# The weights of the first w1 chunk behind w2, placed 32 bytes nearer to x modulo 256

## The chip, the cores and the metric

The kernel runs on one core of a Trainium2 chip. Its time is the device time of one execution in microseconds (us); the runs shown are compared by their median. The engines of a core work side by side: TensorE (PE; its loading of weights is shown apart, as PEld), VectorE (DVE), ScalarE (ACT), GpSimd (POOL) and SyncE (SP), which issues the transfers.

## What is computed

Two transformer layers over 256 tokens of width 2048 in float32. The first layer's mixer is stick-breaking attention, the second's a sparse attention in three branches; behind each mixer stands the same kind of MLP with a hidden width of 8192. The MLPs are what this change touches:

```python
def sqrelu_mlp(h, w1, w2):
    return jnp.square(jax.nn.relu(h @ w1)) @ w2
...
h = h + sqrelu_mlp(rms_norm(h, mlp_norm_g[layer]), mlp_w1[layer], mlp_w2[layer])
```

## The kernel before

**Products in three parts.** Float32 products are made from parts. Each operand is split into a rounded part `hi` and the rest `lo`, and a product is the sum of three: hi by hi, lo of the activations by hi of the weights, and hi of the activations by lo of the weights. `split` (line 129 on) makes the parts of a chunk of weights: a chunk is 128 x 1024 elements (512 KB), ScalarE copies it into `hi` (line 133), VectorE subtracts (line 135). Activations of the running layer stand in `xs`, with the parts `xhi` and `xlo` side by side; the MLP's hidden values stand in `yhi` and `ylo`.

**Two forms of a chunk.** `chunk_T` (matmul at line 185) loads the weights' parts into TensorE and streams x beside them, 256 columns at a time: 16 matmuls with hi, then 8 with lo. `chunk_N` (line 155) does it the other way round: activations are loaded, and the weights' parts are streamed, 512 columns at a time, 12 matmuls a chunk. `chunk_S` (line 246) is a variant of the second with 256 columns that forms sums of blocks first (one level of Strassen's scheme), 21 matmuls a chunk. In all forms TensorE loads the stationary operand of the next matmul while the moving operand of the running one streams.

**Place modulo 256.** A buffer of parts has `KC * NB + PAD` = 1024 + 64 elements in each partition, 4352 bytes, that is 17 x 256, and a row of `xs` has 2048 bytes. So all buffers of a kind have one place modulo 256 bytes, whichever buffer and whichever column block it is. In the memory map of the compiled program x, yhi, ylo and the starts of the buffers for hi and lo all lie at 128 modulo 256. The offset given to `split` moves the parts inside their buffers: `NEAR` (0 elements, for chunk_N) leaves them at 128, at x's own place; `FAR` (16 elements, 64 bytes, for chunk_T) puts them at 192; `SUM` (48 elements, for chunk_S) at 64.

**Order of the MLP.** `mlp` goes through four groups `fg` of 2048 hidden values. `group1` computes h times w1 for the group: four blocks `fb` of 512 hidden values, each with eight chunks in the form chunk_T, so 192 matmuls of 256 columns a block and 768 a group. `group2` adds the group's part of the product with w2: 24 chunks in the form chunk_N and 8 in the form chunk_S between them. Group 0's w1 stands behind the mixer's output projection, and transposes for the next activations run between its chunks (lines 303 and 352). Groups 1 to 3 stand directly behind the w2 products of the group before. This is done twice, once in each layer, so there are six turns from w2 to w1.

**What sets the order.** Each engine goes through its instructions in the order of the program; buffers come free in turn (five for raw weights, four each for hi and lo). Transfers of weights are issued on SP's queue in the order of the chunks.

Of the kernel before, what the change touches and what calls it, by code (L numbers as in the profile page):

```python
# [18 lines left out]
D = 2048  # L19
KD = D // P  # L20
NB = 512
# [4 lines left out]
KC = 2  # L26
# [13 lines left out]
def hybrid_kernel(  # L40
# [62 lines left out]
    def spawn(gen, rate, wait=0.0, first=False):  # L103
        beside.insert(0 if first else len(beside), [gen, rate, -wait])

    def pump():
        if beside:
            b = beside[0]
            b[2] += b[1] / KC
            while b[2] >= 1:  # L110
                b[2] -= 1
                y = next(b[0], b)
                if y is b:
                    beside.remove(b)
                if y:
                    break
# [6 lines left out]

    PAD = 64
    NEAR, FAR, SUM = 0, 16, 48

    def split(raw, o=(NEAR, NEAR)):
        n = KC * NB  # L130
        view = lambda t, a: t[:, a:a + n].rearrange("p (k n) -> p k n", k=raw.shape[1])
        hi = view(whi.tile([P, n + PAD], F32R, tag="hi", name="hi"), o[0])
        nc.scalar.activation(hi, raw, AF.Copy)  # L133
        lo = view(wlo.tile([P, n + PAD], F32R, tag="lo", name="lo"), o[1])
        nc.vector.tensor_tensor(lo, raw, hi.bitcast(F32), op=OP.subtract)  # L135
# [9 lines left out]
    def load_split(*where, o=(NEAR, NEAR)):  # L145
        return split(load(*where), o)

    def bank(pool, tag):
        return pool.tile([P, NB], F32, tag=tag, name=tag)
# [27 lines left out]
    def chunk_T(ps, src, k0, n0, first, last, nk=KC, o=None):  # L177

        nm = KC * NB // P // nk
        hi, lo = src if isinstance(src, tuple) else load_split(src, k0, nk, n0, nm * P, o=o or (FAR, FAR))  # L180
        tiles = [(kk, m) for kk in range(nk) for m in range(nm)]

        def mm(w, x, kk, m, s, e):
            o = ps[m // 2][:, (m % 2) * T:(m % 2 + 1) * T]
            nc.tensor.matmul(o, w[:, kk, m * P:(m + 1) * P], x[:, k0 + kk, :], start=s, stop=e, skip_group_check=True)  # L185

        for kk, m in tiles:
            mm(hi, xhi, kk, m, first and kk == 0 and m % 2 == 0, False)
            mm(hi, xlo, kk, m, False, False)
        pump()  # L190
        for kk, m in tiles:
            mm(lo, xhi, kk, m, False, last and kk == nk - 1)
        pump()

    def proj_T(ps, src, n0, nk=KC, o=None):
        for k0 in range(0, KD, nk):
            chunk_T(ps, src, k0, n0, k0 == 0, k0 + nk == KD, nk, o)

    def proj_Th(src, n0):

# [10 lines left out]
    def chunk_S(ps, src, k0, n0, first, last, ahi, alo, shi, slo, koff=0):  # L211
# [9 lines left out]
        hi, lo = [  # L221
            wsum.tile([P, 3 * W + PAD], F32R, tag=n, name=n, bufs=1)[:, SUM:SUM + 3 * W] for n in ("shi", "slo")
        ]
# [62 lines left out]
    def split_evac(hi, lo, src, scale=None):  # L286

        if scale is None:
            nc.scalar.activation(hi, src, AF.Copy)  # L289
            nc.vector.tensor_tensor(lo, src, hi.bitcast(F32), op=OP.subtract)  # L290
        else:
            nc.scalar.activation(hi, src, AF.Copy, scale=scale)
            nc.vector.scalar_tensor_tensor(
                lo, src, scale, hi.bitcast(F32), op0=OP.mult, op1=OP.subtract
            )
# [44 lines left out]
    def make_rstd(layer):  # L340
        s = small.tile([P, NT], F32, tag="ms", name="ms")
        nc.vector.tensor_reduce(s, ssq_t[layer], axis=AX.X, op=OP.add)
        nc.vector.tensor_scalar(s, s, 1.0 / D, EPS, op0=OP.mult, op1=OP.add)
        r = small.tile([P, NT], F32, tag="rstd", name="rstd")
        nc.gpsimd.tensor_tensor(r, s, neghalf[:, :NT], op=OP.pow)
        return r

    def bcast_rows(rstd):

        ps = bank(att, "att")  # L350
        for t in range(NT):
            nc.tensor.transpose(ps[:, t * P:(t + 1) * P], rstd[:, t:t + 1].to_broadcast([P, P]), ident)
        return ps
# [36 lines left out]
    def mlp(l, layer, junk, done, last=None):  # L390
        w1, w2 = mlp_w1[l], mlp_w2[l]
        ss = junk.tile([P, 2, KD // 2, 4, P], F32R, name="ss", bufs=1)
        row = junk.tile([P, T], F32, name="row", bufs=1)

        def rows():
            yield
            pb = bcast_rows(make_rstd(layer))
            nc.scalar.activation(row, pb[:, :T], AF.Copy)

        def group1(fg, pools):  # L400

            for fb in range(D // NB):
                ps = [bank(*pools[fb % 2]) for _ in range(NB // P // 2)]
                proj_T(ps, w1, fg * D + fb * NB)
                k, n = fb * (NB // P), NB // P
                a = junk.tile([P, n, T], F32, tag="pre", name="pre", bufs=1)
                for j in range(0, n, 2):
                    nc.vector.scalar_tensor_tensor(
                        a[:, j:j + 2, :], ps[j // 2].rearrange("p (m t) -> p m t", m=2), 0.0,
                        row.unsqueeze(1).to_broadcast([P, 2, T]), op0=OP.max, op1=OP.mult,  # L410
                    )
                s = junk.tile([P, n, T], F32, tag="sq", name="sq", bufs=1)
                nc.scalar.activation(s, a, AF.Square)
                nc.scalar.activation(yhi[:, k:k + n, :], s, AF.Copy)
                nc.vector.tensor_tensor(ylo[:, k:k + n, :], s, yhi[:, k:k + n, :].bitcast(F32), op=OP.subtract)

                sv = s.rearrange("p (j kk) t -> p j kk t", kk=2)
                a1, a2 = [[sv[:, :, kk, t * P:(t + 1) * P] for kk in (1, 0)] for t in range(NT)]
                q = junk.tile([P, 2, 4, P], F32, tag="sums", name="sums", bufs=1)
                nc.vector.scalar_tensor_tensor(q[:, :, 0, :], a2[0], -1.0, a2[1], op0=OP.mult, op1=OP.subtract)  # L420
                nc.vector.tensor_tensor(q[:, :, 2, :], a1[0], a2[0], op=OP.subtract)
                nc.vector.tensor_tensor(q[:, :, 1, :], a2[1], q[:, :, 2, :], op=OP.subtract)
                nc.vector.tensor_tensor(q[:, :, 3, :], a1[1], q[:, :, 1, :], op=OP.subtract)
                split_evac(ss[:, 0, k // 2:k // 2 + 2], ss[:, 1, k // 2:k // 2 + 2], q)

        def group2(fg, plain, strassen, end):

            NK = KD // KC
            order, si = [], 0
            for i in range(3 * NK):  # L430
                order.append(((0, 1, 3)[i // NK], i % NK))
                if si < NK and i >= (3 + 1.75 * si if end else 4 + 2.25 * si):
                    order.append((2, si))
                    si += 1
            for nb, i in order:
                k0 = fg * KD + i * KC
                args = (w2, k0, nb * NB, i == 0, i == NK - 1, yhi, ylo)
                if nb == 2:
                    if i == 0:
                        bs, s = banks_S(*strassen)  # L440
                    chunk_S(s, *args, ss[:, 0], ss[:, 1], koff=fg * KD)
                    if i == NK - 1:
                        add_S(nb, bs, s, junk)
                        if end:
                            for n in range(3):
                                done(n, strassen)
                    continue
                if i == 0:
                    ps = [bank(*plain) for _ in range(NT)]
                out = last is not None and end and nb == 3  # L450
                chunk_N(ps, w2, k0, nb * NB, i == 0, i == NK - (2 if out else 1), yhi, ylo, koff=fg * KD,
                        by_token=out and i == NK - 1)
                if i == NK - 1:
                    if out:
                        add_out(nb, ps, last)
                        return
                    add_h(nb, ps)
                    if end and nb == 3:
                        done(nb, plain)

        spawn(rows(), 1)
        A, B = (acc, "acc"), (att, "att")
        for fg in range(DFF // D):
            end = fg == DFF // D - 1
            group1(fg, ((A, B), (B, A))[fg % 2])
            group2(fg, *((A, B), (B, A))[fg % 2], end)
# [211 lines left out]
    with tc.tile_pool(name="nsa", bufs=2) as ap, ExitStack() as last:  # L678
# [255 lines left out]
        for i in range(2):  # L934
            cT = cp.tile([P, G, T], F32, tag="cT", name="cT", bufs=1)
            for b in range(2):
                ps = proj_Th(w_in, C0 + i * NB + b * T)
# [61 lines left out]
        for g in range(G):  # L999
            ps = [bank(acc, "acc") for _ in range(NT)]  # L1000
# [16 lines left out]
            ps = proj_N(w_in, g * NB)  # L1017
# [46 lines left out]
```

## Time and profile before

| | |
|---|---|
| median of three runs | 2195.87 us (2195.24 to 2197.57) |
| profiled execution | 2196.84 us, span 2195.1 us |
| mean granted clock of TensorE | 0.999 of full speed |
| TensorE busy | 2186.2 us in 14482 matmuls |
| VectorE, ScalarE busy | 1484.1 us, 1164.7 us |
| read from HBM | 401.83 MB |

The span goes from the first to the last instruction; the profiled execution's own time is 1.74 us longer. Times in the rows below are counted from the span's start. A matmul is shown with its whole duration, from issue to the landing of its result, and the next begins long before it ends; how fast a run of matmuls goes is read from the distance between their starts.

### The profile page before, as it was taken

To read this page: it belongs to the slowest core of one execution; us is meant where nothing else is said; L and a number is where in the kernel's file an instruction comes from. 1 tells how busy PE (TensorE), PEld (TensorE's weight loads), DVE (VectorE), ACT (ScalarE), POOL (GpSimd) and SP (SyncE) were. 2 spreads that over 40 slices of the span, in tenths; PEclk is the share of its full clock that TensorE was granted. 3 is DMA by queue.
4 is the path that set the end of the run, shared out by engine and by line. 5 is a ranking of instruction groups with operands and counts; after the bars stand their busy time and mean duration, and the time that the engine had idled before them with its cause. 6 is when DMAs were issued, how large, how long until landed. Compare 5 with 4: busy or idle time off the path is not lost.

```text
span 2195.1 us, 36040 instructions
## 1 busy us (share of the span) xinstructions
PE 2186.2 (100%) x14482; PEld 1997.6 (91%) x14482; DVE 1484.1 (68%) x1968; ACT 1164.7 (53%) x1537; POOL 42.5 (2%) x75
## 2 busy tenths in 40 slices
PE   9999999999999999999999999999999999999999
PEld 9999988998998998899898888889989989989998
DVE  4655556677667667767777877755776676677676
ACT  5555565455445454445546666655544454554453
POOL 0000000000000000000000011000000000000000
PEclk9999999999999999999999999999999999999999
DMA  6655555665665765665667554456657656656654
GB/s 222 204 180 172 156 182 176 186 197 186 200 190 175 215 187 178 215 185 184 203 182 222 163 144 139 139 164 186 190 189 206 182 192 202 191 183 205 189 186 160
DMA packets 260784, 406.28 MB, mean 185 GB/s; under 512 B 13188, under 2 KB 91912, under 8 KB 260616
## 3 DMA queue, kind: packets, MB, share of 16 engines
q1 hardware_dynamic: 259800, 403.52, 60.0%
q8 instruction: 113, 1.85, 0.3%
q10 hardware_dynamic: 816, 0.46, 0.1%
q14 instruction: 55, 0.45, 0.1%
HBM read 401.83 MB, written 2.10 MB: 184 GB/s over the span
## 4 chain that ended last, share of the span: by engine, by line
PE 99%; DVE 0%; POOL 0%; ACT 0%; issue 0%; DVEq 0%; ACTq 0%; POOLq 0%
PE acc L155 31%; PE acc L185 26%; PE att L185 16%; PE att L155 13%; PE acc L246 4%; PE att L246 4%; PE att L896 1%; PE att L303 1%; PE att L888 0%; PE att L889 0%; PE att L890 0%; PE att L583 0%; PE att L631 0%; PE att L842 0%; PE att L844 0%; PE att L843 0%
## 5 line engine op out<-in xcount | busy, mean ns | idle before, releaser
L133 ACT ACTIVATE hi<-raw 128x1024 fp32r<-128x1024 f32 x687 | 726.5, 1059 | 740.3 <-PE acc L155 227.1
L135 DVE TENSOR_TENSOR lo<-raw,hi 128x1024 fp32r<-128x1024 f32 x687 | 836.0, 1221 | 395.6 <-ACT hi L133 374.7
L185 PE MATMUL acc<-xs,hi 128*128 128x256 f32 x3312 | 420.4, 280 | 1.9 <-ACT hi L133 1.9
L185 PEld LDWEIGHTS acc<-xs,hi 128*128 128x128 f32 x3312 | 400.1, 189 | 2.7 <-ACT hi L133 2.1
L185 PE MATMUL att<-xs,hi 128*128 128x256 f32 x2048 | 259.8, 280 | 0.0
L155 PE MATMUL acc<-hi,yhi 128*128 128x512 f32 x640 | 250.7, 392 | 0.0
L155 PE MATMUL acc<-hi,ylo 128*128 128x512 f32 x640 | 249.3, 390 | 0.0
L185 PEld LDWEIGHTS att<-xs,hi 128*128 128x128 f32 x2048 | 248.3, 189 | 0.3
L185 PE MATMUL acc<-xs,lo 128*128 128x256 f32 x1656 | 226.5, 279 | 0.0
L185 PEld LDWEIGHTS acc<-xs,lo 128*128 128x128 f32 x1656 | 207.4, 189 | 0.0
L155 PE MATMUL acc<-hi,xs 128*128 128x512 f32 x704 | 177.2, 392 | 0.0
L155 PE MATMUL acc<-lo,yhi 128*128 128x512 f32 x640 | 172.4, 390 | 0.0
L155 PEld LDWEIGHTS acc<-hi,xs 128*128 128x128 f32 x704 | 130.3, 188 | 26.6
L155 PE MATMUL att<-hi,yhi 128*128 128x512 f32 x380 | 148.2, 390 | 0.0
L155 PE MATMUL att<-hi,ylo 128*128 128x512 f32 x380 | 147.9, 389 | 0.0
L155 PEld LDWEIGHTS acc<-lo,yhi 128*128 128x128 f32 x640 | 119.5, 188 | 24.9 <-issue 0.4
L155 PEld LDWEIGHTS acc<-hi,ylo 128*128 128x128 f32 x640 | 120.2, 188 | 23.3 <-DVE ylo L290 0.2
L155 PEld LDWEIGHTS acc<-hi,yhi 128*128 128x128 f32 x640 | 120.2, 188 | 23.3 <-ACT yhi L289 0.2
L185 PE MATMUL att<-xs,lo 128*128 128x256 f32 x1024 | 140.4, 280 | 0.0
L185 PEld LDWEIGHTS att<-xs,lo 128*128 128x128 f32 x1024 | 128.7, 189 | 0.0
L220 DVE TENSOR_TENSOR ts<-raw 128x512 f32<-128x512 f32 x64 | 44.3, 692 | 115.6 <-DMA raw<-in_mlp_w_dram 115.5
L133 ACT ACTIVATE hi<-ts 128x1024 fp32r<-128x1024 f32 x64 | 67.8, 1059 | 87.8 <-DVE ts L226 41.8
(290 smaller groups left out, 2501.3 us busy)
## 6 DMA issues: line engine op xcount, KB each, us to landing
raw<-in_mlp_w_dram SPq DMA_DIRECT2D x512, 512.0 KB, 3.9
raw<-in_sb_w_qkv_dram SPq DMA_DIRECT2D x95, 512.0 KB, 3.8
raw<-in_nsa_w_in_dram SPq DMA_DIRECT2D x50, 512.0 KB, 3.8
raw<-in_sb_w_out_dram SPq DMA_DIRECT2D x32, 512.0 KB, 3.9
raw<-in_nsa_w_in_dram SPq DMA_DIRECT2D x64, 256.0 KB, 3.4
raw<-in_nsa_w_out_dram SPq DMA_DIRECT2D x32, 512.0 KB, 3.7
w1t<-in_nsa_cmp_w_dram SPq DMA_DIRECT2D x8, 512.0 KB, 4.9
h<-in_x_dram SPq DMA_DIRECT2D x8, 256.0 KB, 4.1
```

What stands on the lines that cost most here:

```text
L133: nc.scalar.activation(hi, raw, AF.Copy)
L135: nc.vector.tensor_tensor(lo, raw, hi.bitcast(F32), op=OP.subtract)
L155: mm = lambda a, b, k, t, s, e: nc.tensor.matmul(ps[t], a[:, k, t * P:(t + 1) * P], b, start=s, stop=e)
L185: nc.tensor.matmul(o, w[:, kk, m * P:(m + 1) * P], x[:, k0 + kk, :], start=s, stop=e, skip_group_check=True)
L220: nc.vector.tensor_tensor(ts[:, :2, :], flat[:, W:3 * W].rearrange("p (a n) -> p a n", a=2), b12, op=OP.subtract)
L246: nc.tensor.matmul(ps[i], a, w, start=s, stop=e, skip_group_check=True)
L303: nc.tensor.transpose(ps[:, j * T + t * P:j * T + (t + 1) * P], h[:, t, (kp + j) * P:(kp + j + 1) * P], ident)
L896: nc.tensor.transpose(ptp[:w, j * P:(j + 1) * P], src(j), ident)
```

## The change

`proj_T` can now give its first chunk another offset, `TURN`: 8 elements, 32 bytes, in place of 64. `group1` asks for it in block 0 of groups 1 to 3. So in six chunks of the whole kernel (three in each layer), hi and lo begin at 160 modulo 256 in place of 192, with x at 128. The chunks behind it, and all others, keep their offsets. No instruction is added or left out.

```diff
-    NEAR, FAR, SUM = 0, 16, 48
+    NEAR, FAR, TURN, SUM = 0, 16, 8, 48
...
-    def proj_T(ps, src, n0, nk=KC, o=None):
+    def proj_T(ps, src, n0, nk=KC, turn=False):
         for k0 in range(0, KD, nk):
-            chunk_T(ps, src, k0, n0, k0 == 0, k0 + nk == KD, nk, o)
+            o = TURN if turn and k0 == 0 else FAR
+            chunk_T(ps, src, k0, n0, k0 == 0, k0 + nk == KD, nk, (o, o))
...
                 ps = [bank(*pools[fb % 2]) for _ in range(NB // P // 2)]
-                proj_T(ps, w1, fg * D + fb * NB)
+                proj_T(ps, w1, fg * D + fb * NB, turn=fg > 0 and fb == 0)
```

## Rows read from the trace of the kernel before

**Rows 1.** The page, part 1: busy time, share of span, number of instructions.
```profile
PE 2186.2 (100%) x14482; PEld 1997.6 (91%) x14482; DVE 1484.1 (68%) x1968; ACT 1164.7 (53%) x1537; POOL 42.5 (2%) x75
```

**Rows 2.** Table of waits, TensorE: who was waited for, total, times, longest.
```profile
PE acc L185 <- ACT hi L133: 1.9, 1, 1.9
PE att L489 <- POOL ident masks.py:199: 1.6, 1, 1.6
PE att L761 <- DVE hs L757: 0.9, 1, 0.9
PE att L796 <- DVE kc L792: 0.5, 1, 0.5
PE acc L508 <- ACT hi L501: 0.2, 1, 0.2
```

**Rows 3.** Chain that ended last, by time: start, duration, what, number of matmuls.
```profile
421.39 21.76 PE att L185 x192
...
571.76 22.61 PE att L185 x192
...
2083.42 22.61 PE acc L185 x192
```

**Rows 4.** Windows of w1 stages, line 185: length, busy (number), granted clock, DMA.
```profile
412.96:486.51 73.55, 73.55 (x649) 73.51 (x648) 1.00 0.66 193
571.60:662.05 90.45, 90.45 (x768) 90.41 (x767) 1.00 0.65 190
...
1505.68:1579.23 73.55, 73.55 (x649) 73.52 (x648) 1.00 0.65 194
...
2015.42:2105.87 90.45, 90.45 (x768) 90.41 (x767) 1.00 0.65 189
```

**Rows 5.** Timeline at the first turn: start, duration, engine, line, count.
```profile
570.69 1.07 PE L155 MATMUL acc<-lo,yhi 128*128 128x512 f32 x4
...
571.60 2.05 PE L185 MATMUL att<-xs,hi 128*128 128x256 f32 x16
573.48 1.11 PE L185 MATMUL att<-xs,lo 128*128 128x256 f32 x8
```

**Rows 6.** Timeline of TensorE in the first w1 stage.
```profile
400.92 2.05 PE L185 MATMUL acc<-xs,hi 128*128 128x256 f32 x16
402.80 1.11 PE L185 MATMUL acc<-xs,lo 128*128 128x256 f32 x8
...
406.93 0.60 PE L303 MATMUL att<-ident,h 128*128 128x128 f32 x4
...
410.10 1.98 PE L185 MATMUL acc<-xs,hi 128*128 128x256 f32 x16
411.92 1.07 PE L185 MATMUL acc<-xs,lo 128*128 128x256 f32 x8
```

**Rows 7.** Timeline of TensorE at the end of the kernel, line 163.
```profile
2190.08 0.40 PE L163 MATMUL att<-lo,yhi 128*128 128x256 f32 x2
2190.32 0.40 PE L163 MATMUL att<-hi,yhi 128*128 128x256 f32 x2
2190.56 0.40 PE L163 MATMUL att<-hi,ylo 128*128 128x256 f32 x2
```

**Rows 8.** The page, part 5: splitting a chunk; busy, mean ns, idle before.
```profile
L133 ACT ACTIVATE hi<-raw 128x1024 fp32r<-128x1024 f32 x687 | 726.5, 1059 | 740.3 <-PE acc L155 227.1
L135 DVE TENSOR_TENSOR lo<-raw,hi 128x1024 fp32r<-128x1024 f32 x687 | 836.0, 1221 | 395.6 <-ACT hi L133 374.7
```

**Rows 9.** Window of the first w1 stage, all engines: PE, PEld, DVE, ACT, POOL.
```profile
412.96:486.51 73.55, 73.55 (x652) 73.55 (x649) 48.58 (x54) 38.32 (x39) 0.00 (x0) 1.00 0.66 193
```

**Rows 10.** Window of 32 matmuls of compress, line 750.
```profile
1199.17:1202.95 3.78, 3.78 (x32) 3.73 (x31) 1.00 0.66 164
```

**Rows 11.** Timeline of TensorE, a projection of the first layer behind chunk_N.
```profile
153.74 1.07 PE L155 MATMUL acc<-lo,xs 128*128 128x512 f32 x4
154.64 2.05 PE L185 MATMUL acc<-xs,hi 128*128 128x256 f32 x16
156.53 1.11 PE L185 MATMUL acc<-xs,lo 128*128 128x256 f32 x8
```

**Rows 12.** Timeline of TensorE behind the products with tri and ones.
```profile
103.05 0.28 PE L618 MATMUL att<-sh,tri 128*128 128x256 f32 x1
103.16 0.28 PE L619 MATMUL att<-sl,tri 128*128 128x256 f32 x1
103.28 1.98 PE L185 MATMUL acc<-xs,hi 128*128 128x256 f32 x16
105.09 1.07 PE L185 MATMUL acc<-xs,lo 128*128 128x256 f32 x8
106.00 1.18 PE L185 MATMUL acc<-xs,hi 128*128 128x256 f32 x9
```

**Rows 13.** Timeline of TensorE behind the products with the values.
```profile
114.48 1.19 PE L185 MATMUL acc<-xs,lo 128*128 128x256 f32 x8
115.51 2.05 PE L185 MATMUL acc<-xs,hi 128*128 128x256 f32 x16
117.39 1.11 PE L185 MATMUL acc<-xs,lo 128*128 128x256 f32 x8
```

**Rows 14.** Timeline of TensorE, first products of w2 behind two w1 stages.
```profile
486.51 0.40 PE L155 MATMUL acc<-hi,yhi 128*128 128x512 f32 x1
...
487.89 0.39 PE L155 MATMUL acc<-hi,yhi 128*128 128x512 f32 x1
...
662.05 0.40 PE L155 MATMUL att<-hi,yhi 128*128 128x512 f32 x1
...
663.44 0.39 PE L155 MATMUL att<-hi,yhi 128*128 128x512 f32 x1
```

## The prediction

> **What bounds the kernel now.** I read the page's busy times first: TensorE is busy for 2186.2 of 2195.1 us [rows 1]. The table of waits then says whether that is real. All that TensorE's matmuls waited for another engine is 1.9, 1.6, 0.9, 0.5 and 0.2 us, 5.1 us together [rows 2]. So nothing that feeds TensorE can give more than those 5 us, and the kernel's time is the number of matmuls times the distance between the starts of two of them. I call that distance the pace. It has to be read from starts, not from the duration of one matmul, because matmuls overlap.
>
> The third view is the chain that ended last, in order of time [rows 3]. One block of w1 is always 192 matmuls of 256 columns at line 185. The reader is to compare equal work: blocks of the first w1 stage take 21.76 us (113.3 ns a matmul), blocks of a later stage 22.61 us (117.8 ns). [...]
>
> The fourth view is the timeline where a pace begins. At the turn from w2 to w1 the first 16 matmuls behind the last product of w2 take 573.48 - 571.60 = 1.88 us, 117.5 ns each [rows 5]: the slow pace is there from the first chunk, and by [rows 4] it stays for all 32 chunks. In the first stage the same line starts slow as well (400.92 to 402.80, 16 in 1.88 us), but transposes stand between its chunks; after them it is fast, 16 in 1.82 us (410.10 to 411.92) [rows 6], and it stays fast to the end of that stage. The pace is thus a rhythm that the stage inherits: it survives as long as identical chunks follow each other, and a disturbance can change it.
>
> **The change part by part.** No instruction is added, removed or moved: the same 24 matmuls, one Copy on ScalarE and one subtraction on VectorE for each chunk. What changes is the start of hi and lo in six chunks (three turns in each of two layers): 160 modulo 256 in place of 192, with x at 128. The distance between the weights that are loaded and the x that streams beside them goes from 64 to 32 bytes; the other 31 chunks of each stage keep 64.
>
> *Does the distance matter at all?* The rows say yes. At the very end of the kernel matmuls of the same shape run with a distance of 0 (line 163, weights and moving data both at 128). Their pairs start at 2190.08, 2190.32 and 2190.56 [rows 7]: 120 ns each, constant, at the same clock. At a distance of 64 the steady paces are 113.3 and 117.8. [...]
>
> [...]
>
> *Work on ScalarE and VectorE.* A chunk's Copy is 1059 ns and its subtraction 1221 ns [rows 8] for the same 1024 elements at either place. I cost the move at nothing. The cover: in a fast stage a chunk lasts 24 x 113.3 = 2.72 us, and ScalarE is busy 38.32 and VectorE 48.58 of 73.55 us [rows 9]. Were the cover gone, only what exceeds 2.72 us would show; that is over a microsecond away. Transfers: a faster stage asks for its 512 KB every 2.72 us in place of 2.83. The first stages do exactly that, at 193 GB/s against 190, without TensorE idling [rows 4, 9].
>
> *The chunk with the new distance.* The trace has no long run at a distance of 32. The nearest are the matmuls of compress (line 750), whose weights step through eight distances, 32 among them: 32 of them in a row take 3.78 us, 118.1 ns on the mean [rows 10]. So I bound the six chunks by 113.3 and 120 ns and take 117.8, what they have now: 0 us, between -6 x 24 x 4.45 ns = -0.6 us and 6 x 24 x 2.2 ns = +0.3 us.
>
> *The 31 chunks behind it.* This is the only term of size. If the return from 32 to 64 leaves the stage at the fast pace, a stage saves 31 x 24 x 4.45 ns = 3.31 us, and six save 19.9 us; take some 0.1 us off for matmuls in which the new pace settles (after transposes it takes two or three). That is 19.8 us. From below it is 0, if the 117.8 ns come back.
>
> Which end is nearer? Entries into line 185 in the trace: straight from a long run of 512-column products the pace is slow each time (571.60 [rows 5], 154.64 [rows 11], and all six turns by [rows 4]). But entered without a pause from a few 256-column matmuls at a distance of 0, it is fast: 16 in 1.81 us (103.28 to 105.09), then the 8 of lo in 0.91 [rows 12]. After a pause it is mostly fast [rows 6], sometimes slow: behind the value products 16 take 1.88 us (115.51 to 117.39) [rows 13]. So the long 512-column run is the one entry that never gives 113.3 ns, and what the change does is to put 24 matmuls of 256 columns with another distance between that run and the stage. That is nearer to [rows 12] than to [rows 5], and I take the fast end, without being sure of it: a disturbance re-rolls the rhythm, and [rows 13] shows that it can fall on 117.8.
>
> *Behind the stage.* The first six products of w2 take 487.89 - 486.51 = 1.38 us behind a fast stage and 663.44 - 662.05 = 1.39 us behind a slow one [rows 14]. So the gain isn't given back there, and w2's own pace does not depend on it.
>
> **Sum.** 2196.84 us for the profiled execution, less 19.8, is 2177.0. The median of the runs shown is 2195.87, 0.97 lower, so I forecast 2195.87 - 19.8 = 2176.1 us.
>
> **The rivals.**
> *The 117.8 ns come back.* [...] For it: six of six turns, and the entry behind a pause in [rows 13]. Against it: [rows 12]. Price: the bounds of the six chunks alone, -0.6 to +0.3 us: 2195.9 us. Chance 0.25.
>
> *The change doesn't do what it says*: the place has no effect on pace and the two paces come from something else, such as the phase of two clocks. Then even the six chunks keep 117.8: 2195.9 us. [...] Against it stands the 120 ns at distance 0 [rows 7]. Chance 0.05.
>
> *Some turns flip, others not.* Each is worth 3.3 us; three of six give 2195.9 - 9.9 = 2186.0. For it: pauses of the same kind in [rows 6] and [rows 13] end differently. Against it: all six turns behave alike in [rows 4]. Chance 0.07.
>
> *Slower:* the chunk at 32 leaves a third rhythm, as slow as line 163's 120 ns, and the stage inherits it. Price: 6 x 31 x 24 x 2.2 ns = 9.8 us, 2205.7 us; it decides from a pace of 118.8 on, where 4464 matmuls lose 4.4 us. For it: 120 ns holds steadily at the end of the kernel [rows 7]. Against it: at a distance of 64 the long stages show two paces only, and these 31 chunks have a distance of 64. Chance 0.04.
>
> **How the numbers follow.** My forecast has 0.59: 2174.6 to 2178.5 by its own bounds (all of the first chunk's gain on the best run, against some late settling and the spread of runs). The partial case adds 0.07 and reaches to 2190. To leave out no more than 2 in 10 the range has to take in the return of the 117.8 ns, 2195.9 with the spread of the runs: 2174.6 to 2197.4. 0.2% is 4.4 us, about what a measurement of this kernel can tell from no change. Faster: 0.59 + 0.07 = 0.66. Same: 0.25 + 0.05 = 0.30. Slower: 0.04.
>
> **What would show it.** In the chain of the changed kernel the later w1 blocks of 192 should take 21.76 us, and their windows about 87.1 us in place of 90.45. The timeline at a turn should show 16 matmuls in about 1.81 us from the second or third chunk on. Blocks of 22.61 us mean that the first rival holds; a first chunk at an unchanged 117.8 ns would speak for the second; 23 us and more for the last. The w2 stages and the first w1 stage must be unchanged; if their lengths move, my account of what the change touches is wrong. The prediction fails if the rhythm behind the chunk is set by something that 24 matmuls at another distance don't alter.

## The result, and the profile after

The changed kernel takes 2177.06 us (median of four runs, 2175.53 to 2177.46), the kernel before, run beside it, 2196.72 us (2195.24 to 2199.73): a ratio of 0.9907, 95% interval 0.989 to 0.9925, so 0.9% faster. The forecast was 2176.1 us. The profiled execution has a span of 2175.3 us against 2195.1, 19.8 us less.

The page's busy times, part 1, of the changed kernel: the numbers of instructions are the same, and TensorE is busy for 20.8 us less [rows 1].

```profile
PE 2165.4 (100%) x14482; PEld 1976.4 (91%) x14482; DVE 1482.8 (68%) x1968; ACT 1163.2 (53%) x1537; POOL 42.6 (2%) x75
```

The chain that ended last, in order of time, at the first and the last turn. All lines are one higher than before: line 186 is the former 185.

```profile
570.38 21.88 PE att L186 x192
592.26 21.76 PE acc L186 x192
614.02 21.76 PE att L186 x192
635.78 21.76 PE acc L186 x192
...
1998.71 21.88 PE att L186 x192
...
2064.11 21.76 PE acc L186 x192
```

Every block that took 22.61 us [rows 3] now takes 21.76 us, but for the first of each stage, which holds the chunk at 32 bytes. The windows of the w1 stages, line 186 alone:

```profile
411.46:485.01 73.55, 73.55 (x649) 73.51 (x648) 1.00 0.66 193
570.22:657.38 87.16, 87.16 (x768) 87.12 (x767) 1.00 0.67 199
742.48:829.64 87.16, 87.16 (x768) 87.12 (x767) 1.00 0.67 197
...
1998.55:2085.71 87.16, 87.16 (x768) 87.12 (x767) 1.00 0.65 193
```

All six stages are 87.16 us long. Two of the six windows of before stand in [rows 4]; these are the other four:

```profile
747.15:837.60 90.45, 90.45 (x768) 90.41 (x767) 1.00 0.65 190
922.69:1013.15 90.46, 90.46 (x768) 90.41 (x767) 1.00 0.64 187
...
1664.33:1754.78 90.45, 90.45 (x768) 90.41 (x767) 1.00 0.66 190
1839.87:1930.33 90.46, 90.46 (x768) 90.41 (x767) 1.00 0.65 190
```

So each stage is 3.29 or 3.30 us shorter than before, 19.76 us together. The first w1 stage, which the change does not touch, is 73.55 us as before; the granted clock is 1.00 in all these windows, before and after. That accounts for the 19.8 us of the span. (Outside the stages this execution was 1.4 us ahead at the first turn and lost 1.3 us again later: 0.9 us in the w2 products behind the second layer's first w1 stage, most of the rest behind the last stage.)

The timeline of TensorE at the first turn, to be held against [rows 5]:

```profile
569.31 1.08 PE L156 MATMUL acc<-lo,yhi 128*128 128x512 f32 x4
570.22 2.06 PE L186 MATMUL att<-xs,hi 128*128 128x256 f32 x16
572.12 1.11 PE L186 MATMUL att<-xs,lo 128*128 128x256 f32 x8
573.06 1.98 PE L186 MATMUL att<-xs,hi 128*128 128x256 f32 x16
574.88 1.07 PE L186 MATMUL att<-xs,lo 128*128 128x256 f32 x8
```

The chunk at 32 bytes takes 573.06 - 570.22 = 2.84 us for its 24 matmuls, 118.3 ns each: a little more than the 117.8 ns that it had. The chunk behind it goes at the short pace at once, 16 in 574.88 - 573.06 = 1.82 us. So nothing is gained where the place was changed; all is gained in the 31 chunks behind it, whose place was not changed.

### The profile page after: what moved, and what is told of

Same layout as the page of the kernel before. It is cut to its first block, busy times and chain, and to the rows that moved or that the text cites. A ratio compares the mean times of both kernels' runs of the same rounds, so it can differ in the third digit from the quotient of the medians.

```text
span 2175.3 us, 36040 instructions
## 1 busy us (share of the span) xinstructions
PE 2165.4 (100%) x14482; PEld 1976.4 (91%) x14482; DVE 1482.8 (68%) x1968; ACT 1163.2 (53%) x1537; POOL 42.6 (2%) x75
## 4 chain that ended last, share of the span: by engine, by line
PE 97%; DMA 1%; DVE 1%; issue 0%; POOL 0%; ACT 0%; DVEq 0%; ACTq 0%; POOLq 0%
PE acc L156 29%; PE acc L186 26%; PE att L186 16%; PE att L156 13%; PE acc L248 4%; PE att L248 3%; DMA raw<-in_mlp_w_dram 1%; PE att L898 1%; DVE lo L136 1%; PE att L305 1%; PE att L890 0%; PE att L891 0%; PE att L892 0%; PE att L585 0%; PE att L633 0%; PE att L844 0%
## 5 line engine op out<-in xcount | busy, mean ns | idle before, releaser
L186 PE MATMUL acc<-xs,hi 128*128 128x256 f32 x3312 | 413.5, 277 | 1.9 <-ACT hi L134 1.9
L186 PEld LDWEIGHTS acc<-xs,hi 128*128 128x128 f32 x3312 | 393.5, 188 | 2.8 <-ACT hi L134 2.1
L186 PE MATMUL att<-xs,hi 128*128 128x256 f32 x2048 | 253.3, 276 | 0.0
L186 PEld LDWEIGHTS att<-xs,hi 128*128 128x128 f32 x2048 | 242.2, 188 | 0.3
```

## The experiments

Three theories stood at first. A "break" is here a short stretch of matmuls that differ from those around them. A (rhythm): 113.3 and 117.8 ns are two rhythms of the same matmuls, and any break can move the stage from one to the other. B (place): 32 bytes is the better distance in itself. C (seam): what counts is how the first weights are loaded beside the last product of w2. Each run was made once, beside the kernel before on the same chip, whose time is given in brackets; the verdicts rest on the length of the six stages in the trace, which agree within 0.02 us in all runs but one.

**All chunks at 32 bytes.**

```diff
-            o = TURN if turn and k0 == 0 else FAR
+            o = TURN if turn else FAR
...
-                proj_T(ps, w1, fg * D + fb * NB, turn=fg > 0 and fb == 0)
+                proj_T(ps, w1, fg * D + fb * NB, turn=fg > 0)
```

> All 32 chunks of the six w1 stages behind w2 have the 32 byte distance, not the first alone. Theory A (rhythm): the two paces at a distance of 64 are two rhythms of one thing, 32 is no better distance in itself and only breaks the rhythm. Then the whole stage keeps the pace that the first chunk of the changed kernel has, 2.84 us for 24 matmuls (118.2 ns): 90.8 us a stage, about 2199 us in all. Theory B (place): 32 is the better place. Then the stage is at 113.3 ns or less, 87.0 us a stage, 2176.5 us or less.

2198.34 us (2193.31). The window of the first stage behind a turn, line 186, and the chain of this kernel, second and third block of that stage:

```profile
570.23:661.11 90.88, 90.88 (x768) 90.83 (x767) 1.00 0.64 189
...
593.11 22.72 PE acc L186 x192
615.83 22.72 PE att L186 x192
```

118.3 ns from the first matmul of a stage to the last, more than before the change. B is refuted: 32 bytes is no better distance, it only leads to something better at 64.

**The second chunk in place of the first.**

```diff
-            o = TURN if turn and k0 == 0 else FAR
+            o = TURN if turn and k0 == nk else FAR
```

> The second chunk of each of the six stages has the 32 byte distance, the first keeps 64. Theory A (rhythm): the first chunk runs at 117.8 ns, the second at about 118, from the third on 113.3: 87.3 us a stage, about 2177.8 us. Theory C (seam): what counts is how the very first weights are loaded beside the last product of w2 (that product took 235 ns in place of 226 in the changed kernel). Then nothing is gained: 90.45 us a stage, about 2197 us.

2174.29 us (2193.31). The window of its first stage behind a turn, line 186, and the timeline of TensorE there, three chunks:

```profile
567.96:655.24 87.28, 87.28 (x768) 87.24 (x767) 1.00 0.65 198
...
567.96 2.05 PE L186 MATMUL att<-xs,hi 128*128 128x256 f32 x16
569.84 1.10 PE L186 MATMUL att<-xs,lo 128*128 128x256 f32 x8
570.78 2.06 PE L186 MATMUL att<-xs,hi 128*128 128x256 f32 x16
572.67 1.11 PE L186 MATMUL att<-xs,lo 128*128 128x256 f32 x8
573.62 1.99 PE L186 MATMUL att<-xs,hi 128*128 128x256 f32 x16
575.45 1.07 PE L186 MATMUL att<-xs,lo 128*128 128x256 f32 x8
```

The first chunk, with the seam as it was before, runs at 117.5 ns (16 in 1.88 us), the third at 113.3 or little more; all six stages are 87.28 us. C is refuted: the break works behind the seam too, with the first chunk as it was.

**A distance of 0 in the first chunk, and in all chunks.**

```diff
-            o = TURN if turn and k0 == 0 else FAR
+            o = NEAR if turn and k0 == 0 else FAR
```

> The first chunk of the six stages has a distance of 0 in place of 32. Theory A (rhythm): any other distance will do as a break; the chunk itself runs at 120 ns as line 163 did, the 31 behind it at 113.3: 87.2 us a stage, about 2177.3 us. Theory B (32 is special): the 117.8 ns come back behind it, 90.5 us a stage, about 2197 us.

The second kernel has `NEAR if turn` and `turn=fg > 0`, so that all 32 chunks of the six stages are at 0.

> All 32 chunks of the six stages at a distance of 0. If the distance between the two reads sets the pace, each stage runs at line 163's 120 ns, 92.1 us, and the kernel takes 2196.8 + 6 x 1.7 = 2207 us. [...]

With 0 in the first chunk 2196.2 us (2193.31); timeline of TensorE at its first turn:

```profile
570.48 2.08 PE L186 MATMUL att<-xs,hi 128*128 128x256 f32 x16
572.39 1.12 PE L186 MATMUL att<-xs,lo 128*128 128x256 f32 x8
573.35 2.05 PE L186 MATMUL att<-xs,hi 128*128 128x256 f32 x16
575.23 1.10 PE L186 MATMUL att<-xs,lo 128*128 128x256 f32 x8
```

The chunk at 0 runs at about 120 ns (573.35 - 570.48 = 2.87 us for 24), and behind it 16 take 1.88 us again. Theory A as I had written it, that any other distance will do, is refuted: behind 24 matmuls at 0 the 117.8 ns come back, in all six stages (90.50 us each). With 0 in all chunks 2203.7 us (2197.38); the window of its first stage behind a turn, line 186:

```profile
568.20:660.35 92.15, 92.15 (x768) 92.10 (x767) 1.00 0.64 188
```

92.15 us for 768 matmuls are 120.0 ns, what line 163 showed [rows 7]. The place alone moves the stage to 92.15 us, from the 87.16 us of the changed kernel or the 90.45 us of the kernel before, at the same clock.

These runs move the weights and leave x where it is, so by themselves they don't tell whether the distance counts or the place of the weights alone. The kernel before has a pair that does: line 163 and chunk_S both load from 128 (yhi and ylo, chunk_S also their sums), but line 163 streams parts that stand at 128 and chunk_S parts that stand at 64. The first takes 120 ns a matmul, the second 117.8 (21 matmuls in 2.473 us, in the median of its 64 chunks, from the single records). So the place of the streamed data counts too, which speaks for the distance; no run moved x itself. Nor does a run show that the places repeat every 256 bytes and no sooner. What the trace shows is that the buffers of hi, 4352 bytes (17 x 256) apart, do not differ: from the third chunk on, each chunk of the six stages before has a mean of 117.75 to 117.79 ns a matmul (from the single records).

**A transpose ahead of the stage, all chunks at 64.**

```diff
                 ps = [bank(*pools[fb % 2]) for _ in range(NB // P // 2)]
+                if fg > 0 and fb == 0:
+                    nc.tensor.transpose(ps[0][:, :P], ident, ident)
```

> The kernel before with all chunks at 64, and one transpose of the identity ahead of each of the six stages, into the bank that the first matmul of the stage clears (its result is not used). Theory A (rhythm): a break of any kind can do it, as the transposes do in the first stage: 113.3 ns after a few matmuls, about 0.3 us for the break, 87.4 us a stage, about 2178.5 us. Theories B and C as far as they need another place: 90.45 us a stage and 0.1 to 0.3 us for the transpose, about 2198 us.

2183.61 us (2193.31). The chain of this kernel, the second block behind the first, second and third turn (its lines are those of the kernel before):

```profile
590.58 21.76 PE acc L185 x192
...
763.68 22.61 PE att L185 x192
...
938.52 21.76 PE acc L185 x192
```

Four of the six stages went to the short pace (87.14 and 87.15 us), the second of each layer stayed at 117.8 ns (90.54 us). So no other place is needed for the gain, and a break is not sure to bring it. This is the partial case among my rivals, by another means. Which turns flip is the same in both layers.

**96 bytes in the first chunk.**

```diff
-    NEAR, FAR, TURN, SUM = 0, 16, 8, 48
+    NEAR, FAR, TURN, SUM = 0, 16, 24, 48
```

> The first chunk of the six stages has a distance of 96, as far from 64 as 32 is, on the other side. After the run with a distance of 0 theory A is narrowed: a chunk breaks the rhythm if it leaves an uneven one of its own, as 32 does (single starts 115 to 123 ns apart), and not if it runs evenly, as 0 does. Theory A: 96 is uneven too, and the stage behind it is at 113.3 ns, about 87.2 us a stage, 2177 us. Theory B (32 alone, or the side nearer to x): the 117.8 ns come back, 90.5 us, 2197 us.

2180.73 us (2197.38), all six stages 87.14 or 87.15 us; the chain at the first turn, first and second block:

```profile
570.10 21.86 PE att L186 x192
591.97 21.76 PE acc L186 x192
```

It works on the other side of 64 as well; nearness to x is not what counts. (The time is 3.7 us above that of the changed kernel though the stages are no longer. Most of it lies behind the first layer's last w1 stage: in the chain it is 1092.20 - 958.21 = 133.99 us from that stage's third block to the first long piece at line 186 of the second layer, and 1089.98 - 958.54 = 131.44 in the changed kernel. Single times differ by such stretches, so the stages are compared.)

**How many matmuls it takes.** Five kernels change which matmuls at the head of a stage have 32 bytes. The first gives lo of the first chunk another place than hi:

```diff
-            chunk_T(ps, src, k0, n0, k0 == 0, k0 + nk == KD, nk, (o, o))
+            chunk_T(ps, src, k0, n0, k0 == 0, k0 + nk == KD, nk, (FAR, o))
```

> In the first chunk of the six stages hi keeps 64 and only lo, the last 8 matmuls, has a distance of 32. Theory A: the uneven rhythm shows within a few matmuls, so eight are enough: 16 at 117.8, 8 at about 118, then 113.3: 87.15 us a stage, 2177 us. If the break needs a full chunk to build up, some or all stages stay at 90.45 us.

2194.83 us (2197.38): all six stages 90.46 us, no gain. The chain, first and second block behind the first turn:

```profile
568.49 22.62 PE att L186 x192
591.10 22.61 PE acc L186 x192
```

The four others have hi of the first chunk at 32 bytes (`(o, FAR)`), both of the first two chunks (`k0 <= nk`), the first chunk with hi of the second, and lo of the first chunk with all of the second.

> In the first chunk of the six stages only hi, the first 16 matmuls, has a distance of 32; lo keeps 64. After the run in which the last eight matmuls alone had 32 and all six stages stayed at 117.8 ns, two readings are left. Length: eight matmuls are too few for the new rhythm to settle, more are enough. Moment: the 32 byte rhythm is uneven, and it depends on where in it the return to 64 falls whether the stage takes 113.3 or 117.8 ns. Length: 16 is between the 8 that failed and the 24 that worked, 87.1 us a stage if it is enough. Moment: either 87.1 or 90.45 us.

> The first two chunks, 48 matmuls, have a distance of 32. Length: 113.3 ns from the third chunk on in all six stages, 87.28 us a stage, 2177.8 us. Moment: either that, or 117.8 ns behind them, 90.5 us a stage, 2197 us.

> The first chunk and hi of the second, 40 matmuls, have a distance of 32. Length: 113.3 ns behind them, 87.25 us a stage, 2177.6 us. Moment: either that or 90.5 us a stage, 2197 us, and it may differ from the run with 48 matmuls.

> lo of the first chunk and all of the second, 32 matmuls, have a distance of 32; the same entry as in the run with eight, which left the stages at 117.8 ns, but 24 matmuls more. Length: 113.3 ns from the third chunk on, 87.28 us a stage, 2177.8 us. Moment: either that or 90.5 us a stage, 2197 us.

In this order 2174.28, 2177.84, 2176.59 and 2195.47 us (2195.53). The chain, first and second block behind the first turn, of the kernel with 16 matmuls:

```profile
568.59 21.84 PE att L186 x192
590.43 21.76 PE acc L186 x192
```

and of the one with 32, entered at the seventeenth matmul:

```profile
570.34 22.63 PE att L186 x192
592.97 22.61 PE acc L186 x192
```

| matmuls at 32 bytes | which | stage, us | pace behind them |
|---|---|---|---|
| 8 | 17 to 24 | 90.46 | 117.8 |
| 16 | 1 to 16 | 87.12 | 113.3 |
| 24 (the change) | 1 to 24 | 87.16 | 113.3 |
| 24 | 25 to 48 | 87.28 | 113.3 |
| 32 | 17 to 48 | 90.47 | 117.8 |
| 40 | 1 to 40 | 87.24 | 113.3 |
| 48 | 1 to 48 | 87.28 | 113.3 |

Length does not decide: 32 matmuls fail where 16, 24, 40 and 48 succeed. What the table does show is that both breaks that begin at the seventeenth matmul fail and all that begin at the first or the twenty-fifth succeed. The distances from start to start (ns, worked out from the single records of the trace; the bar stands where the first matmul at 64 bytes starts) at the first turn:

```
1 to 16    121 116 116 120 117 122 118 115 | 115 113 113 114 113
1 to 24    122 115 116 120 117 122 118 116 | 114 113 114 113 113
1 to 40    122 116 116 120 116 123 117 116 | 114 114 113 113 114
1 to 48    122 115 116 120 117 122 118 116 | 114 113 114 113 113
17 to 24   116 121 118 117 117 122 116 115 | 120 117 118 118 117
17 to 48   120 116 123 117 117 122 115 116 | 119 118 118 118 117
25 to 48   118 116 122 116 116 120 116 120 | 119 121 115 115 114
first chunk at 0   120 120 120 120 120 120 120 118 | 118 118 117 119 117
```

At 32 bytes the starts settle after some eight matmuls and then repeat every eight (122 116 116 120 117 122 118 116, to within 1 ns, 118.3 ns on the mean; with all chunks at 32 the whole stage is like that). Entered at the first matmul, all counts that a chunk or half a chunk allows are multiples of eight, so the return to 64 always falls on the same point of the period, and it is a good one. Entered at the seventeenth, it falls three starts further in the period, behind 122 116 116, and the 117.8 ns come back. Entered at the twenty-fifth it falls on a third point, behind 120 116 120, and 113.3 ns are reached after four starts. So of the points of the period that were met two are good and one is not. At 0 one start is like the other, and the one point that there is was not good.

That the point of the return decides is a reading that fits all these runs, but they don't show it. Since every count is a multiple of the period, the point of the return is fixed by the point of the entry, and no run changes the one without the other; that the entry at the seventeenth matmul, where lo takes over from hi, is the bad thing fits as well. A break of, say, 20 matmuls would tell them apart and was not tried. Nor must a break be made of whole periods: at 96 bytes the starts repeat about every five (118 117 119 117 115 118 116 121 117 114), which 24 matmuls do not fill evenly, and all six stages went to 113.3 ns.

**The same break in chunk_S.** In the changed kernel the parts shi and slo get an offset of 56 elements in place of 48.

```diff
-            wsum.tile([P, 3 * W + PAD], F32R, tag=n, name=n, bufs=1)[:, SUM:SUM + 3 * W] for n in ("shi", "slo")
+            wsum.tile([P, 3 * W + PAD], F32R, tag=n, name=n, bufs=1)[:, SUMT:SUMT + 3 * W] for n in ("shi", "slo")
```

> The changed kernel, and in each of the 64 chunks in the form chunk_S the first six matmuls of hi and three of lo (the parts shi and slo) have a distance of 32 in place of 64; the other 12 keep 64. These chunks start at 2.47 us each (117.7 ns). Theory A: the break works there as well, the matmuls behind it go to 113.3 ns: up to 8 + 4 of 21 gain 4.45 ns, 0.05 us a chunk, 3 us in all, less what the entry into the 512 column products costs from the fast rhythm (232 and 236 ns for the first two in place of 227, about 0.015 us a chunk, 1 us): 2175 us. If a chunk of 21 is too short for the new rhythm to settle, no change: 2177 us, or up to 2 us more.

2177.46 us (2197.38), against 2177.06 for the changed kernel: no gain. In this kernel's timeline the matmuls behind the changed ones keep the old distance, for instance six sums from 499.41 to 500.11:

```profile
499.41 0.87 PE L248 MATMUL att<-hi,ss 128*128 128x256 f32 x6
500.11 0.28 PE L248 MATMUL att<-hi,yhi 128*128 128x256 f32 x1
```

0.70 us for six are 117 ns. In the median a chunk in the form chunk_S takes 2.480 us in this run and 2.473 in the changed kernel (from the single records), so there is a small loss and no gain. Whether six matmuls are the wrong moment or chunk_S has no shorter rhythm was not tried.

## Why the prediction was right

*What bounds the kernel.* Right: what was gained is TensorE's pace. Stages of either pace have a granted clock of 1.00, with a DMA share of 0.64 to 0.66 before and 0.65 to 0.67 after, and TensorE is busy in all of each, so neither clock nor supply makes the difference. The 4.45 ns of the sum are the distance of the two paces in [rows 4]: 90.45 us / 768 = 117.77 ns less 73.55 us / 649 = 113.33 ns is 4.44 ns.

*Does the distance matter.* Right, and shown with whole stages: 120.0 ns at 0, 118.3 at 32, 113.3 or 117.8 at 64. A stage takes 90.45 us with its chunks at 64 and 92.15 us with its chunks at 0, with nothing else changed and the granted clock at 1.00 in both. By what means the distance acts is not seen in the trace. The rival that the change doesn't do what it says falls.

*The chunk with the new distance.* I took 117.8 ns within 113.3 to 120; it is 118.3. Six chunks lose about 0.07 us together.

*The 31 chunks behind it.* 19.8 us forecast, 19.76 measured in the six stages (3.29 or 3.30 each). The settling that I put at 0.1 us is smaller: at the first turn the first distance behind the return is 114 ns, the next 113.

*Why the short pace was likelier.* The outcome was right, the reason only half. I leaned on [rows 12], an entry from a few 256-column matmuls at distance 0 that led to 113.3 ns. A whole chunk at 0 does not (2196.2 us). What holds is the other sentence, that a disturbance can fall on either side: the transposes gave four of six, and 8 or 32 matmuls from the seventeenth on gave none. Nothing in the prediction's rows told that these 24 matmuls would fall on the good side, so that they did was in part luck: with the same break at lo of the first chunk, or with a distance of 0, the first rival (117.8 ns come back) would have been the result. Five of the seven breaks at 32 bytes that were tried gave the short pace.

*The partial case and the slower one.* All six turns behave alike in every run but the one with the transpose. There the second turn of each layer stays slow although it too comes out of 512-column products, so a like entry is no full account. A third rhythm was not inherited anywhere: behind 0, 32 and 96 bytes the stages at 64 had 113.3 or 117.8 ns, nothing else.

*Behind the stage* nothing is given back, as read from [rows 14]: the distance from the end of a changed stage to the next turn is as before but for 0.01 us (829.64 to 914.74 now, 837.60 to 922.69 before, 85.10 and 85.09). The prediction wanted all w2 stages unchanged. One moved by 0.9 us, the one behind the second layer's first w1 stage (the others by less than 0.4). These are its windows before and after, and a line of the changed kernel's table of waits that [rows 2] does not have:

```profile
1579.23:1664.33 85.10, 85.10 (x459) 73.85 (x458) 65.28 (x82) 42.93 (x44) 0.00 (x0) 1.00 0.60 195
...
1568.03:1654.03 86.00, 85.36 (x459) 73.90 (x457) 65.31 (x83) 42.40 (x44) 0.00 (x0) 1.00 0.58 192
...
PE att L248 <- DVE slo L229: 0.6, 1, 0.6
```

TensorE is idle in it for 0.64 us, and the line names a wait for a part of chunk_S. The change does not by itself make that wait: the same stage took 86.01 us with lo alone at 32 bytes, where the w1 stages kept 90.46 us, and 85.10 with 16 matmuls at 32, where they became short. What brings it was not followed up.

What stays open is why there are two rhythms at all: the trace gives the start of each load and each matmul and nothing finer. Nor is it shown why one break leads to 113.3 ns and another to 117.8.

## What to carry to other kernels

Compare equal blocks of the same line along the kernel: where clock, suppliers and shapes agree and the pace does not, the stage may have inherited a rhythm at its entry, and a few matmuls with the weights at another distance from the moving data may change it (here 144 of 14482 matmuls, at 32 bytes in place of 64, gave 0.9%). Try several such breaks and read all entries in the trace, since a distance that is worse in itself may be the one that leads to the short pace, and a break of a slightly different length may not. Look at the places of weights and moving data too: a distance of 0 cost 120.0 ns for each matmul of 256 columns here, one of 64 bytes 113.3 or 117.8.

## What was not expected of the hardware

At a distance of 32 bytes the starts have a period of eight matmuls (118.3 ns on the mean), at 0 they are all within 1 ns of 120 ns apart. At 64 two paces, 113.3 and 117.8 ns, live side by side without a crossing: in none of the stages of 768 matmuls, in this kernel, the one before or the twelve others, did the pace change once it had settled. And one transpose at the turn is as good a break as a chunk at 32 bytes in four cases of six, the first and the third turn of each layer (87.14 or 87.15 us against 90.54); as both layers agree, chance seems to have little part in it.
